# One layer of a hybrid encoder: the recurrence's products with T and with the scores as 64x64 tiles, the attention values as two 64-column products

## Chip, cores and metric

The kernel runs on one core of a Trainium2 chip. The metric is the device time of one execution in microseconds (us). The profile is of one execution of its own; times are the median of several runs without the profiler.

## What is computed

The layer takes a residual stream of 1024 tokens by 1024 features. One input projection feeds two groups of heads: neighbourhood attention (8 heads of 64) and a gated delta rule in both directions (4 heads of 128, chunks of 64 tokens). Their outputs go through one output projection, and a mixture of 64 small experts follows. The change lies in the last step of the delta rule and in the last product of the attention. The delta rule, for one direction and head, cut to what matters:

```python
def step(state, inp):                      # one chunk of 64 tokens, 16 chunks in turn
    q_c, k_c, u_c, w_c, g_c, qk_c = inp
    v_new = u_c - w_c @ state              # u_c, w_c: solutions of a triangular system
    o_c = (q_c * exp(g_c)) @ state + qk_c @ v_new
    state = state * exp(g_last) + (k_c * exp(g_last - g_c)).T @ v_new
    return state, o_c

out = einsum('bhqrc,rbhqce->bqhe', softmax(logits), v_win)   # attention values
```

## The kernel before

The work before the recurrence projects the inputs, convolves, builds for each of the 16 chunks the inverse T of the triangular matrix (64x64 for each head and direction, kept in DRAM as T_d) and the decayed scores (kept as SA_d). The recurrence then goes through 16 steps n. In step n the forward direction (d=0) takes chunk n and the backward one (d=1) takes chunk 15-n; tokens of d=0 lie on partitions 0 to 63, those of d=1 on partitions 64 to 127. The four heads h lie side by side in the columns.

One step (lines 509 to 567) does this:

- pk (line 529): keys and queries of the chunk times the state st, eight products of 128x128, four for each direction.
- r (line 531, VectorE): values minus the first half of pk, eight instructions on 64 partitions.
- pw (line 536): T times r, four products, one for each head. Both directions go in one product, so T stands in `at[:, 1, h]` as a 128x128 matrix with one 64x64 block for each direction on its diagonal and zeros elsewhere.
- wc (lines 537 and 538): the copy of pw out of PSUM, half by ScalarE, half by VectorE.
- ps (line 545): keys times wc, eight products that use 64 rows of the array each, rows 0 to 63 for d=0 and 64 to 127 for d=1.
- sn (lines 550 and 551): the old state is decayed by GpSimd and VectorE adds ps. This is the next state.
- po (line 559): the scores times wc, four products with the same block-diagonal form (`at[:, 0, h]`), into the buffer of pw. VectorE adds the part from the state (line 563) and GpSimd issues two transfers to on_d (line 565).

A matrix product of float32 operands is run as two passes, so the trace shows two MATMUL records for each of these products. Products of operands of the form float32r take one pass.

The program is written step after step, but a scheduler lays out each engine's instructions. Between the steps of the recurrence it puts the input projection of the other columns (nat_block, lines 84 to 86: three passes of 256 columns for each 128 rows, called fillers below). What is left of that projection follows the recurrence; then the attention begins.

The attention goes through 64 blocks of 128 queries of one head, two blocks (h=0, h=1) for each group of queries. attn_values (line 654 on) forms the product of the values with the transposed weights for both heads at once: the 128 columns of two heads as the stationary operand and 2x128 moving columns, three products summed. Only two of the four quarters of the result are used; two VectorE copies take them (line 665). The output projection (dn_mm2 and ao_mm, lines 84 to 86 again, with 512 columns) is laid between the attention's blocks by the scheduler.

Of the kernel before, what the change touches and what calls it, by code (L numbers as in the profile page):

```python
# [8 lines left out]
F32 = mybir.dt.float32  # L9
# [3 lines left out]
AF = mybir.ActivationFunctionType  # L13
OP = mybir.AluOpType
# [5 lines left out]
P = 128  # L20
# [5 lines left out]
DH, DD = 4, 128  # L26
CH = 64
NCH = S // CH
# [8 lines left out]
def tile_layer(ctx, tc, a, out):  # L37
    nc = tc.nc
    pe, act, dve, pool, sp = nc.tensor, nc.scalar, nc.vector, nc.gpsimd, nc.sync
# [137 lines left out]
    X, T1, T2, BETA, G, GC, EGC, DL, C1, C2 = (gt[:, i] for i in range(10))  # L177
    egl = dnp.tile([P, 2, NCH, DH], F32, name="egl")
# [322 lines left out]
    psK = scn.enter_context(tc.tile_pool(name="psK", bufs=1, space=PSUM, side="right"))  # L501
    hf = [slice(d * 64, d * 64 + 64) for d in range(2)]

    atb = [sc1.tile([P, 2, DH, 2, CH], F32, name=f"at{i}") for i in range(2)]
    for i in range(2):
        pool.memset(atb[i], 0.0)
    st = None
    for n in range(NCH):
        ch = [slice(step(d, n) * CH, step(d, n) * CH + CH) for d in range(2)]
        kn = sc2.tile([P, DH, DD], F32, name="kn")  # L510
        vn = sc2.tile([P, DH, DD], F32, name="vn")
        at = atb[n % 2]
        for d in range(2):
            sp.dma_start(at[hf[d], 1, :, d], T_d[hf[d], n])
            sp.dma_start(vn[hf[d]], v_d[ch[d]])
        for d in range(2):
            sp.dma_start(kn[hf[d]], k_d[ch[d]])
            sp.dma_start(at[hf[d], 0, :, d], SA_d[hf[d], n, :, 1])
        kd = sc2.tile([P, DH, DD], F32, name="kd")
        pool.tensor_tensor(kd, kn, DL[:, n, :, None].to_broadcast([P, DH, DD]), op=OP.mult)  # L520
# [12 lines left out]
        pw = psK.tile([P, DH, DD], F32, name="pw")  # L533
        wc = sc2.tile([P, DH, DD], F32, name="wc")
        for h in range(DH):
            pe.matmul(pw[:, h], at[:, 1, h], r[:, h], start=True, stop=True)
        act.activation(wc[:, 0:2], pw[:, 0:2], AF.Copy)
        dve.tensor_copy(wc[:, 2:4], pw[:, 2:4])
        if n < NCH - 1:
            sn = sc2.tile([P, 2, DH, DD], F32, name="sn")  # L540

            ps = [psK.tile([P, DH, DD], F32, name=f"ps{d}") for d in range(2)]
            for h in range(DH):
                for d in range(2):
                    pe.matmul(ps[d][:, h], kd[hf[d], h], wc[hf[d], h], start=True, stop=True)
            for d in range(2):
                if n == 0:
                    dve.tensor_copy(sn[:, d], ps[d])
                else:
                    pool.tensor_tensor(sn[:, d], st[:, d], egl[:, d, n, :, None].to_broadcast([P, DH, DD]), op=OP.mult)  # L550
                    dve.tensor_tensor(sn[:, d], ps[d], sn[:, d], op=OP.add)
        o = sc2.tile([P, DH, DD], F32, name="o")
        if n > 0:
            for h in range(DH):
                for d in range(2):
                    act.activation(o[hf[d], h], pk[d][hf[1], h], AF.Copy, scale=EGC[hf[d], n, h:h + 1])
        po = psK.tile([P, DH, DD], F32, name="pw")
        for h in range(DH):
            pe.matmul(po[:, h], at[:, 0, h].rearrange("p d c -> p (d c)"), wc[:, h], start=True, stop=True)
        if n == 0:  # L560
            dve.tensor_copy(o, po)
        else:
            dve.tensor_tensor(o, po, o, op=OP.add)
        for d in range(2):
            pool.dma_start(on_d[d, ch[d]], o[hf[d]].rearrange("p h e -> p (h e)"))
        if n < NCH - 1:
            st = sn

# [37 lines left out]
    qks, lgs, bts, pTs = {}, {}, {}, {}  # L606
# [47 lines left out]
    def attn_values(i):  # L654
        half, pr, w, h = blocks[i]
        if h == 0:
            return None

        pv, pT = psQ.tile([P, 2, P], F32, name="pv", bufs=1), pTs.pop(i // 2)
        for g in range(3):  # L660
            pe.matmul(pv, vw[:, w, half + g, pr * P:(pr + 1) * P], pT[:, g], start=(g == 0), stop=(g == 2))  # L661
        av = aTs[half][:, pr].rearrange("p (r c) -> p r c", c=64)[:, :, w * 16:w * 16 + 16]
        for h in range(2):
            hs = slice(h * 64, h * 64 + 64)
            ins = dve.tensor_copy(av[hs], pv[hs, h].rearrange("p (r c) -> p r c", c=16))
        return ins

    def attn_step(i):
        if i < len(blocks):
# [572 lines left out]
```

## Time and profile before

| | us |
|---|---|
| median of 3 runs | 1382.51 (1381.34 to 1383.73) |
| the profiled execution, its time | 1388.08 |
| its span from first to last instruction | 1386.4 |
| PE busy, share of the span | 85% |
| VectorE (DVE), GpSimd (POOL), ScalarE (ACT) busy | 46%, 28%, 27% |

Busy time is an average over stages with different limits. The recurrence lies between 345 and 490 us of the span, the rest of the input projection between 490 and 550, the attention with the output projection between 550 and 765, the router until 825, and the experts behind that. The rows below are from these stages.

### The profile page before, as it was taken

What the parts mean: (1) busy time and instruction counts of PE and PEld (TensorE: products, weight loads), DVE (VectorE), ACT (ScalarE), POOL (GpSimd) and SP (SyncE); (2) the same over time, 40 slices, a digit from 0 to 9 for tenths busy, and PEclk for the clock granted to TensorE, in tenths of its full rate; (3) what the DMA queues carried; (4) which work ended last, traced back from release to release, by engine and by line L of the source; (5) the groups of instructions that cost most, each with busy time, mean ns of one, the idle gap of its engine ahead of it and who ended that gap; (6) DMA issues with size and microseconds to landing.
All of it is one profiled execution on the core that took longest, in us unless ns stands there. A gap on an engine that the chain in (4) does not pass through costs nothing. (4 is left out here: it accounts for less than half of the span.)

```text
span 1386.4 us, 21032 instructions
## 1 busy us (share of the span) xinstructions
PE 1177.5 (85%) x7427; PEld 821.7 (59%) x7428; DVE 643.5 (46%) x1615; ACT 375.8 (27%) x768; POOL 381.9 (28%) x433
## 2 busy tenths in 40 slices
PE   6977999979989896679989968887887788868885
PEld 6866889979889895467768853333332333323332
DVE  5556863763466633667867962122211212122211
ACT  6435432322244423665545310000000000000000
POOL 1147313013567463121210352111212112212111
PEclk9989999988999997899999969999998999989999
DMA  4251246346666497998692979999999999998991
GB/s 160 67 116 48 66 143 166 97 135 137 198 184 163 124 251 199 261 266 206 166 265 104 334 307 357 398 409 400 398 404 397 353 391 406 393 372 333 402 383 54
DMA packets 109954, 347.13 MB, mean 250 GB/s; under 512 B 43104, under 2 KB 49248, under 8 KB 93168
## 3 DMA queue, kind: packets, MB, share of 16 engines
q1 hardware_dynamic: 74480, 260.68, 52.2%
q0 software_dynamic: 27056, 68.79, 19.2%
q10 hardware_dynamic: 8272, 15.78, 3.2%
q8 instruction: 83, 1.36, 0.4%
q14 instruction: 63, 0.52, 0.1%
HBM read 305.26 MB, written 61.67 MB: 265 GB/s over the span
## 5 line engine op out<-in xcount | busy, mean ns | idle before, releaser
L1037 PE MATMUL pp<-wg,xT 128*64 128x512 f32 x1024 | 229.7, 598 | 17.7 <-DVE xT L1026 16.7
L1072 PE MATMUL po<-wd,hT 128*64 128x512 f32 x512 | 128.2, 632 | 44.2 <-DVEq L1151 31.7
L1037 PEld LDWEIGHTS pp<-wg,xT 128*64 128x64 f32 x1024 | 72.3, 137 | 153.3 <-issue 130.4
L84 PE MATMUL pA<-w_hi,h_hi 128*128 128x256 f32 x512 | 151.2, 295 | 0.0
L86 PE MATMUL pA<-w_hi,h_lo 128*128 128x256 f32 x512 | 149.2, 291 | 0.0
L85 PE MATMUL pA<-w_lo,h_hi 128*128 128x256 f32 x512 | 148.9, 291 | 0.0
L1053 POOL DMA_INDIRECT out<-yg,tS x32 | 50.8, 1586 | 287.0 <-DVE yg L1074 243.3
L1041 DVE SCALAR_TENSOR_TENSOR sg<-pp,tS,sg 128x256 f32<-128x256 f32 x32 | 15.5, 484 | 229.9 <-ACTq L1151 185.8
L1072 PEld LDWEIGHTS po<-wd,hT 128*64 128x64 f32 x512 | 42.8, 144 | 129.9 <-issue 67.8
L1074 DVE TENSOR_SCALAR yg<-po,tS 128x512 f32<-128x512 f32 x64 | 46.7, 749 | 125.2 <-DMA out<-yg,tS 62.9
L84 PEld LDWEIGHTS pA<-w_hi,h_hi 128*128 128x128 f32 x512 | 101.1, 197 | 0.4 <-issue 0.2
L85 PEld LDWEIGHTS pA<-w_lo,h_hi 128*128 128x128 f32 x512 | 100.9, 197 | 0.0
L86 PEld LDWEIGHTS pA<-w_hi,h_lo 128*128 128x128 f32 x512 | 100.6, 196 | 0.1
L1040 ACT ACTIVATE sg<-pp,tS 128x256 f32<-128x256 f32 x32 | 15.1, 473 | 267.5 <-PE pp L1037 267.5
L84 PE MATMUL pA<-h_hi,w_hi 128*128 128x512 f32 x192 | 76.7, 399 | 0.0
L85 PE MATMUL pA<-h_lo,w_hi 128*128 128x512 f32 x192 | 76.6, 399 | 0.0
L86 PE MATMUL pA<-h_hi,w_lo 128*128 128x512 f32 x192 | 76.0, 396 | 0.0
L76 DVE TENSOR_TENSOR w_lo<-w_raw,w_hi 128x512 fp32r<-128x512 f32 x56 | 39.1, 714 | 72.6 <-ACT w_hi L75 71.0
L250 DVE SCALAR_TENSOR_TENSOR acc<-raw,convw,acc 128x1024 f32<-128x1024 f32 x48 | 63.2, 1319 | 11.5 <-ACT acc L248 11.1
L1049 ACT ACTIVATE hT<-ph 128x256 f32<-128x256 f32 x32 | 12.3, 384 | 193.4 <-PE ph L1047 193.4
L84 PE MATMUL pA<-wo_hi,t_hi 128*128 128x512 f32 x128 | 55.0, 429 | 7.1 <-ACT t_hi L746 5.3
L661 PE MATMUL pv<-pT,vw 128*128 128x256 f32 x192 | 54.3, 419 | 3.3 <-ACT pT L652 2.4
(338 smaller groups left out, 2329.4 us busy)
## 6 DMA issues: line engine op xcount, KB each, us to landing
wg<-in_w_gu SPq DMA_DIRECT2D x62, 2048.0 KB
wd<-in_w_down SPq DMA_DIRECT2D x63, 1024.0 KB
bt<-in_bias SPq DMA_DIRECT2D x24, 384.0 KB
w_raw<-in_w_nat SPq DMA_DIRECT2D x32, 256.0 KB
w_raw<-in_w_dn SPq DMA_DIRECT2D x24, 256.0 KB
k<-kk_d POOLq DMA_DIRECT2D x16, 384.0 KB
SA_d<-cm POOLq DMA_DIRECT2D x8, 512.0 KB
kk_d<-ev POOLq DMA_DIRECT2D x8, 512.0 KB
```

What stands on the lines that cost most here:

```text
L76: dve.tensor_sub(lo[:, k:k + 2], raw, hi[:, k:k + 2].bitcast(F32))
L84: pe.matmul(dst, sh, mh, start=(i == 0), stop=False)
L85: pe.matmul(dst, sh, ml, start=False, stop=False)
L86: pe.matmul(dst, sl, mh, start=False, stop=(i == n - 1))
L250: dve.scalar_tensor_tensor(acc, raw[:, t:t + S], convw[:, m, t:t + 1], acc, op0=OP.mult, op1=OP.add)
L661: pe.matmul(pv, vw[:, w, half + g, pr * P:(pr + 1) * P], pT[:, g], start=(g == 0), stop=(g == 2))
L1037: pe.matmul(pp[d * CAP:(d + 1) * CAP], xT[:, k, d * CAP:(d + 1) * CAP], ws[d][0][:, :, k * 256:(k + 1) * 256], start=(k == 0), stop=(k == ...
L1040: act.activation(sg[:n], pp[:n, 0], AF.Silu, scale=mf[:n, 3:4])
L1041: dve.scalar_tensor_tensor(sg[:n], pp[:n, 1], mf[:n, 3:4], sg[:n], op0=OP.mult, op1=OP.mult)
L1053: ins = pool.indirect_dma_start(out=out, out_offset=bass.IndirectOffsetOnAxis(ap=idx, axis=0), in_=yg, in_offset=None, bounds_check=S - 1, ...
L1072: pe.matmul(po[d * CAP:(d + 1) * CAP], hT[:, k, d * CAP:(d + 1) * CAP], w[1][:, k * D + c * 512:k * D + (c + 1) * 512], start=(k == 0), st ...
L1074: dve.tensor_scalar(yg[:n, cs], po[:n], mf[:n, 2:3], None, op0=OP.mult)
```

## The change

Three parts.

1. The products with T. T is loaded as it lies in DRAM into tt (one transfer for both directions), and each head and direction has a 64x64 product of its own. Even heads leave the result on the direction's own half of the partitions, odd heads on the other half (`hf[d ^ p]`). The result has two tiles, one for each direction, in two PSUM banks; ScalarE copies the one, VectorE the other. The block-diagonal buffers and their zeroing go.
2. As the odd heads now lie on the other half, the keys (four transfers of half the size in place of two), the scores (four in place of two) and the decay factors (DLs) are laid out so as well. The state products keep their form but are grouped by partition half i; the addition to the state becomes four instructions in place of two, that to o two in place of one, the transfers to on_d four in place of two. The products with the scores become eight of 64x64 in place of four.
3. attn_values forms one product for each head with 64 stationary columns and 128 moving ones, into the two halves of the partitions of one tile, and one copy in place of two.

```diff
-    atb = [sc1.tile([P, 2, DH, 2, CH], F32, name=f"at{i}") for i in range(2)]
-    for i in range(2):
-        pool.memset(atb[i], 0.0)
+    DLs = sc1.tile([P, 2, NCH, 2], F32, name="DLs")
+    for d in range(2):
+        for p in range(2):
+            dve.tensor_copy(DLs[hf[d ^ p], d], DL[hf[d], :, p::2])
...
         for d in range(2):
-            sp.dma_start(at[hf[d], 1, :, d], T_d[hf[d], n])
             sp.dma_start(vn[hf[d]], v_d[ch[d]])
         for d in range(2):
-            sp.dma_start(kn[hf[d]], k_d[ch[d]])
-            sp.dma_start(at[hf[d], 0, :, d], SA_d[hf[d], n, :, 1])
+            for p in range(2):
+                sp.dma_start(kn[hf[d ^ p], d], k_d[ch[d]][:, p::2])
+        for d in range(2):
+            for p in range(2):
+                sp.dma_start(at[hf[d ^ p], d], SA_d[hf[d], n, p::2, 1])
...
-        pw = psK.tile([P, DH, DD], F32, name="pw")
+        pw = [psK.tile([P, 2, DD], F32, name=f"ps{d}") for d in range(2)]
...
         for h in range(DH):
-            pe.matmul(pw[:, h], at[:, 1, h], r[:, h], start=True, stop=True)
-        act.activation(wc[:, 0:2], pw[:, 0:2], AF.Copy)
-        dve.tensor_copy(wc[:, 2:4], pw[:, 2:4])
+            g, p = divmod(h, 2)
+            for d in range(2):
+                pe.matmul(pw[d][hf[d ^ p], g], tt[hf[d], h], r[hf[d], h], start=True, stop=True)
+        act.activation(wc[:, 0], pw[0], AF.Copy)
+        dve.tensor_copy(wc[:, 1], pw[1])
...
-            ps = [psK.tile([P, DH, DD], F32, name=f"ps{d}") for d in range(2)]
-            for h in range(DH):
+            ps = [psK.tile([P, 2, 2, DD], F32, name=f"ps{1 + i}") for i in range(2)]
+            for g in range(2):
                 for d in range(2):
-                    pe.matmul(ps[d][:, h], kd[hf[d], h], wc[hf[d], h], start=True, stop=True)
+                    for i in range(2):
+                        pe.matmul(ps[i][:, d, g], kd[hf[i], d, g], wc[hf[i], d, g], start=True, stop=True)
...
-        po = psK.tile([P, DH, DD], F32, name="pw")
-        for h in range(DH):
-            pe.matmul(po[:, h], at[:, 0, h].rearrange("p d c -> p (d c)"), wc[:, h], start=True, stop=True)
+        po = [psK.tile([P, 2, DD], F32, name=f"ps{2 * i}") for i in range(2)]
+        for g in range(2):
+            for p in range(2):
+                for d in range(2):
+                    i = p ^ d
+                    pe.matmul(po[i][hf[d], g], at[hf[i], d, g], wc[hf[i], d, g], start=True, stop=True)
...
-        pv, pT = psQ.tile([P, 2, P], F32, name="pv", bufs=1), pTs.pop(i // 2)
+        pv, pT = psQ.tile([P, P], F32, name="pv", bufs=1), pTs.pop(i // 2)
         for g in range(3):
-            pe.matmul(pv, vw[:, w, half + g, pr * P:(pr + 1) * P], pT[:, g], start=(g == 0), stop=(g == 2))
+            for h in range(2):
+                hs = slice(h * 64, h * 64 + 64)
+                pe.matmul(pv[hs], vw[:, w, half + g, pr * P + h * 64:pr * P + h * 64 + 64], pT[:, g, h],
+                          start=(g == 0), stop=(g == 2))
```

The scheduler lays the new instructions out anew. On PE, in one step in the middle of the recurrence, the products with T stood so before (pw is their result, pA that of the fillers, and the size behind a name is that of the result):

```order
L536 MATMUL pw_3261<-r_3242,at0_2261 128x128
L84 MATMUL pA_4808<-w_hi_4512,h_hi_73 128x256
L536 MATMUL pw_3261<-r_3242,at0_2261 128x128
L85 MATMUL pA_4808<-w_lo_4513,h_hi_73 128x256
L536 MATMUL pw_3261<-r_3242,at0_2261 128x128 x2
L86 MATMUL pA_4808<-w_hi_4512,h_lo_74 128x256
L84 MATMUL pA_4808<-w_hi_4512,h_hi_73 128x256
```

The last six of the eight products with T of a step of the changed kernel (line 544; they go to ps0 for d=0 and ps1 for d=1), with the state product of line 555 and the score product of line 575 that stand between them:

```order
L544 MATMUL ps0_3108<-r_3089,tt_3074 64x128
L85 MATMUL pA_5072<-w_lo_4591,h_hi_73 128x256
L86 MATMUL pA_5072<-w_hi_4590,h_lo_74 128x256
L544 MATMUL ps1_3109<-r_3089,tt_3074 64x128
L86 MATMUL pA_5072<-w_hi_4590,h_lo_74 128x256
L84 MATMUL pA_5072<-w_hi_4590,h_hi_73 128x256
L85 MATMUL pA_5072<-w_lo_4591,h_hi_73 128x256
L544 MATMUL ps1_3109<-r_3089,tt_3074 64x128
L555 MATMUL ps2_3123<-wc_3110,kd_3087 128x128
L544 MATMUL ps1_3109<-r_3089,tt_3074 64x128
L575 MATMUL ps0_3149<-wc_3110,at_3075 64x128
L544 MATMUL ps1_3109<-r_3089,tt_3074 64x128
```

Products on the whole array, with fillers on the whole array between them, have become products on a quarter of it with the same fillers between them. Over the whole recurrence the 128 products with T (64 before) stand in 109 runs: 94 alone, 13 of two, 2 of four.

Behind the state products of the step, PE stood so before: four score products, and, with a filler between, the eight of the next step's pk.

```order
L545 MATMUL ps0_3199<-wc_3191,kd_3169 128x128
L545 MATMUL ps1_3200<-wc_3191,kd_3169 128x128
L559 MATMUL pw_3222<-wc_3191,at1_2262 128x128 x4
L86 MATMUL pA_4808<-w_hi_4512,h_lo_74 128x256
L529 MATMUL pk0_3243<-sn_3198,qkT_78 128x128 x4
L529 MATMUL pk1_3244<-sn_3198,qkT_78 128x128 x4
```

The same place of the changed kernel (pk is line 535 there):

```order
L555 MATMUL ps2_3030<-wc_3017,kd_2994 128x128
L575 MATMUL ps0_3056<-wc_3017,at_2982 64x128 x3
L84 MATMUL pA_5072<-w_hi_4590,h_hi_73 128x256
L535 MATMUL pk0_3090<-sn_3028,qkT_78 128x128
L85 MATMUL pA_5072<-w_lo_4591,h_hi_73 128x256
L86 MATMUL pA_5072<-w_hi_4590,h_lo_74 128x256
L84 MATMUL pA_5072<-w_hi_4590,h_hi_73 128x256
L85 MATMUL pA_5072<-w_lo_4591,h_hi_73 128x256
L86 MATMUL pA_5072<-w_hi_4590,h_lo_74 128x256
L535 MATMUL pk0_3090<-sn_3028,qkT_78 128x128 x2
L575 MATMUL ps2_3057<-wc_3017,at_2982 64x128 x4
L535 MATMUL pk0_3090<-sn_3028,qkT_78 128x128
```

The score products now stand in two groups, the second between the products pk of the next step. Counted over the recurrence, the 128 score products (64 before) stand in 16 runs of one, 15 of three, 15 of four and one of seven; the 120 state products, before in 15 runs of eight, stand in 14 of one, 14 of seven and one of eight. The number of places at which PE goes from products of one array shape to those of another is 30 before (128 rows by 128 columns to 64 by 128 and back, once in each of 15 steps) and 264 now: 206 between the whole array and 64x64, 14 from the whole array to 64x128, and 44 between 64x64 and 64x128.

In the attention, the value products of one group of queries stood so on PE before (pt are transposes, pq the logits, pA the output projection):

```order
L649 MATMUL pt_6783<-ident_60,lg_6640 128x128 x3
L661 MATMUL pv_6789<-pT_6650,vw_5082 128x256 x3
L635 MATMUL pq_6805<-k2_6466,q2_6465 128x384
L636 MATMUL pq_6805<-kl1_5100,q2_6465 128x384
L84 MATMUL pA_6895<-wo_hi_6730,t_hi_6799 128x512
```

A group of the changed kernel (line 681):

```order
L681 MATMUL pv_6915<-pT_6863,vw_5429 64x128
L84 MATMUL pA_6923<-wo_hi_5862,t_hi_6878 128x512
L85 MATMUL pA_6923<-wo_lo_5863,t_hi_6878 128x512
L84 MATMUL pA_6937<-wo_hi_5862,t_hi_6878 128x512
L681 MATMUL pv_6915<-pT_6863,vw_5429 64x128 x5
```

Three products of one run have become one and then five, with the output projection between. The 192 products (96 before, of 256 columns) stand in 59 runs, 25 of them of one product. Before, neither they nor their neighbours changed the array's shape; now PE goes to 128 rows by 64 columns and back 59 times.

## Rows read from the trace of the kernel before

**Rows 1.** Windows: busy us (count) by engine, granted clock, DMA share, GB/s.

```profile
345.00:490.00 145.00, 132.63 (x1200) 126.19 (x1200) 91.93 (x221) 56.95 (x162) 82.06 (x94) 0.95 0.61 167
...
550.00:765.00 215.00, 184.22 (x887) 147.10 (x887) 152.63 (x547) 124.55 (x267) 35.30 (x53) 0.91 0.81 214
```

**Rows 2.** Waits of PE and of DVE, 345 to 490: total, times, longest.

```profile
PE pk L529 <- DVE sn L551: 5.4, 4, 3.2
...
DVE wc L538 <- ACT wc L537: 14.2, 12, 2.2
```

**Rows 3.** Timeline of PE, one step: start, duration, operation, rows*columns of the array, count.

```profile
449.01 0.39 PE L536 MATMUL pw<-r,at 128*128 128x128 f32 x2
...
450.96 1.16 PE L545 MATMUL ps<-wc,kd 64*128 64x128 f32 x16
452.06 1.16 PE L559 MATMUL pw<-wc,at 128*128 128x128 f32 x8
453.05 1.97 PE L529 MATMUL pk<-sn,qkT 128*128 128x128 f32 x16
...
455.57 0.28 PE L85 MATMUL pA<-w_lo,h_hi 128*128 128x256 f32 x1
455.69 0.28 PE L86 MATMUL pA<-w_hi,h_lo 128*128 128x256 f32 x1
455.81 0.39 PE L536 MATMUL pw<-r,at 128*128 128x128 f32 x2
```

**Rows 4.** Timeline of PE, 450.7 to 451.0: from the fillers to ps.

```profile
450.75 0.28 PE L84 MATMUL pA<-w_hi,h_hi 128*128 128x256 f32 x1
450.96 0.38 PE L545 MATMUL ps<-wc,kd 64*128 64x128 f32 x2
```

**Rows 5.** Timeline of PE, 452.0 to 452.2: from ps to po.

```profile
451.74 0.38 PE L545 MATMUL ps<-wc,kd 64*128 64x128 f32 x3
452.06 0.38 PE L559 MATMUL pw<-wc,at 128*128 128x128 f32 x1
```

**Rows 6.** Timeline of PE, 453.0 to 453.1: from po to pk.

```profile
452.83 0.39 PE L559 MATMUL pw<-wc,at 128*128 128x128 f32 x2
453.05 0.29 PE L529 MATMUL pk<-sn,qkT 128*128 128x128 f32 x1
```

**Rows 7.** Timeline of PE at line 342 (64-column products): 195 to 206, beginning, end.

```profile
197.28 3.71 PE L342 MATMUL pB<-qkT 128*64 128x128 f32 x64
...
196.97 0.38 PE L261 MATMUL pB<-ident,acc 128*128 128x128 f32 x2
197.28 0.33 PE L342 MATMUL pB<-qkT 128*64 128x128 f32 x2
...
200.93 0.50 PE L84 MATMUL pA<-h_hi,w_hi 128*128 128x512 f32 x1
201.26 0.40 PE L85 MATMUL pA<-h_lo,w_hi 128*128 128x512 f32 x1
```

**Rows 8.** The value products: timeline of PE, and the copies (min/median/max ns).

```profile
714.86 1.46 PE L661 MATMUL pv<-pT,vw 128*128 128x256 f32 x6
...
L665 DVE COPY aT<-pv x64: 264/288/297, 555.0 to 761.9; 64x128 f32<-64x128 f32 x64
```

**Rows 9.** Groups, 345 to 490: count, busy us, mean ns, idle before.

```profile
L551 DVE TENSOR_TENSOR sn<-ps,sn 128x512 f32<-128x512 f32 x28 | 18.0, 684 | 8.0 <-PE ps L545 8.0
L538 DVE COPY wc<-pw 128x256 f32<-128x256 f32 x16 | 6.7, 422 | 14.2 <-ACT wc L537 14.2
...
L565 POOL DMA_DIRECT2D on_d<-o x32 | 17.6, 555 | 13.4 <-DVE o L563 6.7 <-issue 6.7
...
L514 SPq DMA_DIRECT2D at<-T_d x32: 573/600/688, 345.9 to 466.2; - x32
```

**Rows 10.** Windows around PE's longest idle time in the recurrence, columns as in Rows 1.

```profile
412.50:415.00 2.50, 0.13 (x1) 0.13 (x1) 1.48 (x3) 1.21 (x2) 0.04 (x1) 0.74 0.74 202
415.00:417.50 2.50, 2.50 (x12) 2.50 (x13) 1.52 (x4) 0.00 (x0) 2.50 (x3) 0.50 0.75 211
```

More of the change, by code (lines that the diff above doesn't have):

```diff
@@ L509, in tile_layer @@
         ch = [slice(step(d, n) * CH, step(d, n) * CH + CH) for d in range(2)]
-        kn = sc2.tile([P, DH, DD], F32, name="kn")
+        kn = sc2.tile([P, 2, 2, DD], F32, name="kn")
         vn = sc2.tile([P, DH, DD], F32, name="vn")
-        at = atb[n % 2]
+        tt = sc2.tile([P, DH, CH], F32, name="tt")
+        at = sc2.tile([P, 2, 2, CH], F32, name="at")
+        sp.dma_start(tt, T_d[:, n])
         for d in range(2):
-            sp.dma_start(at[hf[d], 1, :, d], T_d[hf[d], n])
             sp.dma_start(vn[hf[d]], v_d[ch[d]])
         for d in range(2):
-            sp.dma_start(kn[hf[d]], k_d[ch[d]])
-            sp.dma_start(at[hf[d], 0, :, d], SA_d[hf[d], n, :, 1])
-        kd = sc2.tile([P, DH, DD], F32, name="kd")
-        pool.tensor_tensor(kd, kn, DL[:, n, :, None].to_broadcast([P, DH, DD]), op=OP.mult)
+            for p in range(2):
[3 more added lines that the diff above has]
+                sp.dma_start(at[hf[d ^ p], d], SA_d[hf[d], n, p::2, 1])
+        kd = sc2.tile([P, 2, 2, DD], F32, name="kd")
+        pool.tensor_tensor(kd, kn, DLs[:, :, n, :, None].to_broadcast([P, 2, 2, DD]), op=OP.mult)
         if n == 0:
@@ L532, in tile_layer @@
                                              op0=OP.mult, op1=OP.add)
-        pw = psK.tile([P, DH, DD], F32, name="pw")
-        wc = sc2.tile([P, DH, DD], F32, name="wc")
+        pw = [psK.tile([P, 2, DD], F32, name=f"ps{d}") for d in range(2)]
+        wc = sc2.tile([P, 2, 2, DD], F32, name="wc")
         for h in range(DH):
-            pe.matmul(pw[:, h], at[:, 1, h], r[:, h], start=True, stop=True)
-        act.activation(wc[:, 0:2], pw[:, 0:2], AF.Copy)
-        dve.tensor_copy(wc[:, 2:4], pw[:, 2:4])
+            g, p = divmod(h, 2)
[3 more added lines that the diff above has]
+        dve.tensor_copy(wc[:, 1], pw[1])
         if n < NCH - 1:
             sn = sc2.tile([P, 2, DH, DD], F32, name="sn")
-            ps = [psK.tile([P, DH, DD], F32, name=f"ps{d}") for d in range(2)]
-            for h in range(DH):
+            ps = [psK.tile([P, 2, 2, DD], F32, name=f"ps{1 + i}") for i in range(2)]
+            for g in range(2):
                 for d in range(2):
-                    pe.matmul(ps[d][:, h], kd[hf[d], h], wc[hf[d], h], start=True, stop=True)
[L546 to L552, printed above, removed]
+                    for i in range(2):
+                        pe.matmul(ps[i][:, d, g], kd[hf[i], d, g], wc[hf[i], d, g], start=True, stop=True)
+            for i in range(2):
+                for d in range(2):
+                    sv = sn[:, d, d ^ i::2]
+                    if n == 0:
+                        dve.tensor_copy(sv, ps[i][:, d])
+                    else:
+                        pool.tensor_tensor(sv, st[:, d, d ^ i::2],
+                                           egl[:, d, n, d ^ i::2, None].to_broadcast([P, 2, DD]), op=OP.mult)
+                        dve.tensor_tensor(sv, ps[i][:, d], sv, op=OP.add)
+        o = sc2.tile([P, 2, 2, DD], F32, name="o")
         if n > 0:
@@ L555, in tile_layer @@
                 for d in range(2):
-                    act.activation(o[hf[d], h], pk[d][hf[1], h], AF.Copy, scale=EGC[hf[d], n, h:h + 1])
-        po = psK.tile([P, DH, DD], F32, name="pw")
-        for h in range(DH):
-            pe.matmul(po[:, h], at[:, 0, h].rearrange("p d c -> p (d c)"), wc[:, h], start=True, stop=True)
[L560 to L563, printed above, removed]
+                    act.activation(o[hf[d], h % 2 ^ d, h // 2], pk[d][hf[1], h], AF.Copy, scale=EGC[hf[d], n, h:h + 1])
+        po = [psK.tile([P, 2, DD], F32, name=f"ps{2 * i}") for i in range(2)]
+        for g in range(2):
+            for p in range(2):
+                for d in range(2):
+                    i = p ^ d
+                    pe.matmul(po[i][hf[d], g], at[hf[i], d, g], wc[hf[i], d, g], start=True, stop=True)
+        for i in range(2):
+            if n == 0:
+                dve.tensor_copy(o[:, i], po[i])
+            else:
+                dve.tensor_tensor(o[:, i], po[i], o[:, i], op=OP.add)
         for d in range(2):
-            pool.dma_start(on_d[d, ch[d]], o[hf[d]].rearrange("p h e -> p (h e)"))
+            for p in range(2):
+                pool.dma_start(on_d[d, ch[d]].rearrange("t (g p e) -> t p g e", g=2, p=2)[:, p], o[hf[d], p ^ d])
         if n < NCH - 1:
@@ L657, in attn_values @@
             return None
-        pv, pT = psQ.tile([P, 2, P], F32, name="pv", bufs=1), pTs.pop(i // 2)
+        pv, pT = psQ.tile([P, P], F32, name="pv", bufs=1), pTs.pop(i // 2)
         for g in range(3):
-            pe.matmul(pv, vw[:, w, half + g, pr * P:(pr + 1) * P], pT[:, g], start=(g == 0), stop=(g == 2))
+            for h in range(2):
+                hs = slice(h * 64, h * 64 + 64)
+                pe.matmul(pv[hs], vw[:, w, half + g, pr * P + h * 64:pr * P + h * 64 + 64], pT[:, g, h],
+                          start=(g == 0), stop=(g == 2))
         av = aTs[half][:, pr].rearrange("p (r c) -> p r c", c=64)[:, :, w * 16:w * 16 + 16]
[L663 to L666, printed above, removed]
+        return dve.tensor_copy(av, pv.rearrange("p (r c) -> p r c", c=16))
     def attn_step(i):
```

## Prediction, made before the changed kernel ran

> **What bounds the kernel now.** I read the windows first, to see which stages the change can reach. The recurrence lies in the stretch from 345 to 490 us, the attention in that from 550 to 765 [rows 1]. What follows is started by the attention's end and moves with it. In the recurrence TensorE (PE) is busy 132.6 of 145 us, VectorE (DVE) 91.9, GpSimd 82.1, ScalarE 57.0. So PE idles for only 12.4 us, although the recurrence is a chain of dependent steps: the scheduler has put fillers into the waits. In the attention PE is busy 184.2 of 215.
>
> The waits come next [rows 2]. PE's longest total is 5.4 us for the state. DVE's copy of wc waits 14.2 us in all for ScalarE's copy from the same tile, in 12 of 16 steps. The reader should see two candidates for what sets a step: PE's own sum of work, and the chain T, wc, state, pk, r.
>
> The timeline of one step decides between them [rows 3]. From 449.01 to 455.81 us, 6.80 us, PE runs 8 passes with T, 16 of ps, 8 of po, 16 of pk, and 16 fillers, the last at 455.69. Prices: neighbouring fillers start 0.12 apart; for 128 columns of float32 the last seven of po's eight passes take (1.16 - 0.38) / 7 = 0.11 each [rows 3, 5]. The 14 behind the first two of ps take (1.16 - 0.38) / 14 = 0.056 [rows 3, 4], because the two directions lie on different halves of the array's rows and run side by side. A run of k products whose two passes each share a tile, with neighbours on different tiles, therefore takes about (k + 1) x 0.11.
>
> One price is left, and the whole forecast hangs on it: what PE pays when the array's shape changes. By the ends of the records: the last filler ends at 451.03, and the first two passes of ps, on 64x128, at 451.34, 0.31 later [rows 4], where a pair would need 0.11. Ps ends at 452.12 and the first pass of po, on 128x128 again, at 452.44, 0.32 later [rows 5]. From po to pk, without a change of shape, it is 453.22 to 453.34, 0.12 [rows 6]. At the 64-column products of line 342, the first two end 0.26 behind the transposes before them; at the end it is 200.99 to 201.43, 0.44, where the next pass of 512 columns takes 0.23 [rows 7]. So a change costs 0.20 us, and 0.15 on the way into 64-column products. Now the step adds up: 16 x 0.12 + 8 x 0.11 + 9 x 0.11 + 8 x 0.11 + 16 x 0.11 + 2 x 0.20 = 6.83, against 6.80 measured. PE's own work fills this step.
>
> The Trainium skill says the same of the cause: its page "TensorEngine Tiling (Array Packing)", section "Key Properties", has "Mode switching requires drain", for a change of the tiling mode and not for a change of tile alone; the trace agrees, with 0.32 against 0.12.
>
> **The change part by part.** *Changes of shape in the recurrence.* Before 30, now 264, counted in PE's order: 234 more. At 0.20 each that is 46.8 us. For 44 of them, between 64x64 and 64x128, the trace has no row; free they would leave 190 x 0.20 = 38.0. I take 46.8, since all kinds that are shown pay. A product with T between two fillers now costs a change in, two passes and a change out, 0.62 us in place of 0.22, and the step has no idle time left that could hide it.
>
> *Passes in the recurrence.* T: before 128 passes x 0.11 = 14.1. Now 94 products alone x 0.22 + 13 pairs x 0.33 + 2 runs of four x 0.55 = 26.1: a product of a quarter of the size takes as long as a whole one when nothing stands beside it, and there are twice as many. Po: before 14.1; now 16 x 0.22 + 15 x 0.44 + 15 x 0.55 + 0.88 = 19.3. Ps: before 15 x 0.99 = 14.9; now 14 x 0.22 + 14 x 0.88 + 0.99 = 16.4. Together +18.7.
>
> *What PE's idle time takes up.* A longer step on PE gives the others more time, so waits shrink: 12.4 us at most, nothing at least. I take 9, since part of it stands at the recurrence's start and end.
>
> *A new wait.* One state product and one score product now stand between the last three products with T of d=1, and wait for ScalarE's wc of d=0; behind them on PE are the products for which the whole step waits. The copy takes about 0.42 us (DVE's of that size [rows 9]), and from the last T of d=0 to the first of them PE has three fillers and a T, 3 x 0.12 + 0.62. So nothing; if ScalarE is late by its other work, its lateness counts in each step.
>
> *The other engines in the recurrence.* The addition to the state becomes 56 instructions of 128x256 in place of 28 of 684 ns; at 422 ns, the row of that size, +4.5 us, and the one to o likewise +2.5 [rows 9]. DVE had 53 us to spare. The transfers to on_d double: 32 more x 555 ns = 17.8 us on GpSimd, which had 63 to spare; behind them wait the decay of the state and kd, the next step's work. SP issues 11 transfers a step in place of 8, 48 more x 600 ns = 28.8 us over a stretch that gets longer; the fillers' weights (line 74) stand in the same queue, loaded a block ahead. ScalarE's wc no longer holds DVE's back, as the halves lie in two tiles. That frees up to 14.2 us of the chain, but not of PE, which has work then. All of this is covered by PE's step; without that cover it would be 6.8 on DVE less 14.2.
>
> *Attention.* Passes: before 192 x (1.46 - 0.38) / 5 = 0.216 [rows 8], 41.5 us. Now (192 + 59) x 0.11 = 27.6 (line 342 does 64 passes in 3.71 us, 0.055 each, the same shape [rows 7]). That saves 13.9. The changes of shape take 59 x (0.20 + 0.15) = 20.7. PE: +6.8. DVE loses 32 copies of 288 ns, 9.2 us, and PE does wait for DVE here. Between -9 (PE's idle hides the rest) and +6.8 I take +2.
>
> **Sum.** 46.8 + 18.7 - 9 + 2 = 58.5. The profiled execution took 1388.1 us, so 1446.6. The median of the runs before, 1382.5, is 5.6 lower, and the same shift gives 1441. By the bounds: 38.0 + 18.7 - 12.4 - 9 = +35, 1418; 46.8 + 18.7 + 6.8 = +72, 1455.
>
> **Rivals.** *Faster: the step is set by the chain, and the changes of shape are free beside it.* For it speaks DVE's wait of 14.2 for ScalarE, now gone, and that PE did wait in some steps. Then 18.7 - 12.4 - 13.9 - 14.2 = -22, 1361. It decides where a change of shape costs less than 22 / 352 = 0.06 us (234 in the recurrence, 118 in the attention). Against it: every change in rows 4, 5 and 7 costs at least 0.15, and the step of 6.80 has no idle time in it.
>
> *Four tiles at once.* If the 64x64 products ran four side by side, T and po would take 2 x 256 / 4 x 0.11 = 14.1 in place of 28.2, and with free changes and the attention's 13.9 the time would be near 1382.5 - 14.1 - 13.9 = 1354.5. The order speaks against it: only 34 of the 128 products with T stand beside another one at all. I give this 1 in 100. The Trainium skill, "TensorEngine Tiling (Array Packing)", section "Available Configurations", lists four independent tiles for 64x64; no run here shows four of them in flight.
>
> *Half hidden.* If waits for r, wc or the state fall just before the changes, half of them cost nothing: 23.4 + 18.7 - 9 - 3.6 = +30, 1412.
>
> *Slower still, by the clock.* After PE had been idle for 4 us, the granted clock fell to 0.50, the lower of the two levels, for about 5 us [rows 10]. If the many stops let it fall in a fifth of the recurrence, then some 185 us long, half of 37 us is lost: 1460. Against it: in the dense steps with two changes each it stood at the upper level.
>
> **How the numbers follow.** My forecast 0.78, half hidden 0.08, the clock 0.06, faster 0.05 in all, no change by a sum in between 0.03. The likeliest gives 1441. The range runs from the half hidden case to some way past the clock's: 1405 to 1470. Within 0.2% of the time before is about what a measurement can tell from no change. Slower by more: 0.92; within: 0.03; faster: 0.05.
>
> **What would show it.** In the changed trace a lone product with T between fillers should end 0.3 us behind the filler before it, and the next filler 0.3 behind that; a step should take about 10 us; PE should show no idle time in the recurrence; the attention should last as long as before within 8 us. I am wrong if 64x64 products run beside whole ones, if a step stays near 7 us, or if the copies and additions on DVE, or the transfers on SP, are what PE then waits for.

## The result: 1429.0 us, 3.0% slower, and the profile after

The changed kernel took 1429.01 us, the median of 4 runs (1416.08 to 1435.5), against 1382.69 for the kernel before (4 runs). The ratio is 1.0298, with a 95% interval of 1.0255 to 1.034. The profiled execution took 1431.07 us, its span is 1429.4, 43.0 longer than before, and its mean clock 0.936 (before 0.938).

The first and last instructions of three lines say where the time went. The columns are count, the shortest, median and longest duration, the starts of the first and the last, and the shape.

```profile
L544 PE MATMUL ps<-vn,tt x16: 269/269/320, 358.4 to 359.8; 64*64 64x128 f32 x16
...
L575 PE MATMUL ps<-wc,at x256: 269/269/473, 362.5 to 540.1; 64*64 64x128 f32 x128
...
L681 PE MATMUL pv<-pT,vw x384: 272/273/477, 595.4 to 798.8; 128*64 128x128 f32 x192
```

Before, the first product with T (line 536) began at 360.7, the last score product (line 559) at 486.4, and the value products (line 661) lay between 552.7 and 761.2. So the recurrence went from 126 to 182 us. Some fillers that used to stand behind it moved into it; from the first T to the first value product it is 192.0 before and 237.0 now. **All of the loss lies there, +45 us.** The attention went from 208.5 to 203.4. What follows it took 5 us more. That last stretch took between 625 and 634 us in all the traces of this study, without an order that follows the edits, so I read nothing from it.

The windows (columns as in [rows 1]) show the changed kernel's recurrence, then the stretch from the first T to the first value product, in the changed kernel and in the kernel before.

```profile
358.00:540.00 182.00, 176.76 (x1325) 133.87 (x1327) 94.10 (x260) 54.55 (x158) 101.06 (x145) 0.92 0.45 119
...
358.40:595.40 237.00, 219.72 (x1656) 174.48 (x1655) 114.89 (x316) 67.08 (x180) 132.06 (x183) 0.91 0.58 147
...
360.70:552.70 192.00, 167.32 (x1393) 158.73 (x1394) 109.71 (x275) 68.09 (x182) 107.12 (x122) 0.92 0.71 182
```

In the recurrence PE is busy for 176.8 of 182 us; DVE and GpSimd have 80 us and more to spare. Over the longer stretch PE is busy 52 us more than before and idles 17.3 us in place of 24.7. The granted clock is 0.92 in the recurrence.

The waits in the recurrence (waiting line, what it waited for: total, times, longest):

```profile
DVE wc L546 <- PE ps L544: 41.6, 16, 4.5
...
PE pk L535 <- DVE sn L564: 3.1, 2, 1.6
...
PE ps L544 <- DVE r L537: 1.0, 1, 1.0
```

DVE's wait for ScalarE's copy [rows 2] is gone. Now DVE waits for PE. PE waits for almost nothing.

One step on PE's timeline, 451.89 to 462.62, is 10.73 us long where that of [rows 3] had 6.80:

```profile
451.89 0.43 PE L544 MATMUL ps<-r,tt 64*64 64x128 f32 x2
452.25 0.38 PE L85 MATMUL pA<-w_lo,h_hi 128*128 128x256 f32 x1
452.57 0.43 PE L544 MATMUL ps<-r,tt 64*64 64x128 f32 x2
452.93 0.39 PE L86 MATMUL pA<-w_hi,h_lo 128*128 128x256 f32 x1
453.15 0.28 PE L84 MATMUL pA<-w_hi,h_hi 128*128 128x256 f32 x1
453.26 0.28 PE L85 MATMUL pA<-w_lo,h_hi 128*128 128x256 f32 x1
453.47 0.44 PE L544 MATMUL ps<-r,tt 64*64 64x128 f32 x4
...
455.55 0.48 PE L555 MATMUL ps<-wc,kd 64*128 64x128 f32 x2
455.96 0.32 PE L544 MATMUL ps<-r,tt 64*64 64x128 f32 x1
455.97 0.32 PE L575 MATMUL ps<-wc,at 64*64 64x128 f32 x1
455.97 0.42 PE L544 MATMUL ps<-r,tt 64*64 64x128 f32 x2
456.13 0.27 PE L575 MATMUL ps<-wc,at 64*64 64x128 f32 x1
...
460.19 0.61 PE L535 MATMUL pk<-sn,qkT 128*128 128x128 f32 x4
460.73 0.65 PE L575 MATMUL ps<-wc,at 64*64 64x128 f32 x8
461.31 1.38 PE L535 MATMUL pk<-sn,qkT 128*128 128x128 f32 x10
462.62 0.43 PE L544 MATMUL ps<-r,tt 64*64 64x128 f32 x4
```

Read the ends. A filler ends at 452.25 + 0.38 = 452.63, the lone product with T at 453.00, 0.37 later, and the next filler at 453.32, 0.32 behind that. The two together take 0.69, where without a change of shape they would take 0.22 + 0.12 = 0.34. So, by this reading of the ends, the way into 64x64 costs 0.15, the way out 0.20. The two products of 453.47 also end 0.37 behind the filler before them: two on different quarters of the array take the time of one. From 455.96 two products with T and one with the scores, on three quarters, again end 0.37 behind what stands before them. PE shows no idle time in the step. It holds 23 fillers, where the one before held 16.

### The profile page after: what moved, and what is told of

The parts are those of the page before. It is cut to its first block, busy times and chain, and to the rows that moved or that the text cites. A ratio compares the mean times of both kernels' runs of the same rounds, so it can differ in the third digit from the quotient of the medians.

```text
span 1429.4 us, 22107 instructions
## 1 busy us (share of the span) xinstructions
PE 1230.3 (86%) x7875; PEld 828.1 (58%) x7876; DVE 635.8 (44%) x1633; ACT 372.1 (26%) x766; POOL 404.8 (28%) x491
## 5 line engine op out<-in xcount | busy, mean ns | idle before, releaser
L1055 PE MATMUL pp<-wg,xT 128*64 128x512 f32 x1024 | 233.2, 607 | 21.4 <-DVE xT L1044 21.0
L76 DVE TENSOR_TENSOR w_lo<-w_raw,w_hi 128x512 fp32r<-128x512 f32 x56 | 40.6, 737 | 67.1 <-ACT w_hi L75 65.3
L1067 ACT ACTIVATE hT<-ph 128x256 f32<-128x256 f32 x32 | 12.3, 384 | 192.0 <-PE ph L1065 176.6
L569 ACT ACTIVATE o<-pk,gt 64x128 f32<-64x128 f32 x120 | 35.6, 358 | 80.7 <-PE pk L535 43.8
```

The costliest lines, as they stand in the source:

```text
L76: dve.tensor_sub(lo[:, k:k + 2], raw, hi[:, k:k + 2].bitcast(F32))
L569: act.activation(o[hf[d], h % 2 ^ d, h // 2], pk[d][hf[1], h], AF.Copy, scale=EGC[hf[d], n, h:h + 1])
L1055: pe.matmul(pp[d * CAP:(d + 1) * CAP], xT[:, k, d * CAP:(d + 1) * CAP], ws[d][0][:, :, k * 256:(k + 1) * 256], start=(k == 0), stop=(k == ...
```

## The experiments

In each, the kernel before was run on the same chip, and a ratio is to it.

**The attention's part alone.** The kernel before with the last part of the diff:

```diff
-            pe.matmul(pv, vw[:, w, half + g, pr * P:(pr + 1) * P], pT[:, g], start=(g == 0), stop=(g == 2))
+            for h in range(2):
+                hs = slice(h * 64, h * 64 + 64)
+                pe.matmul(pv[hs], vw[:, w, half + g, pr * P + h * 64:pr * P + h * 64 + 64], pT[:, g, h], ...
```

> The kernel before with the third part alone (attention values as 64-column products, 118 changes of the array's shape in the attention, none more in the recurrence). My account puts the loss into the recurrence: the attention's passes save 13.9 us, the changes cost 118 halves of about 0.35, some of it in PE's idle time, and the trace of the changed kernel shows the attention about 7 us shorter: 1372 to 1384 us. Rival, that the attention bears a good part of the loss: above 1395.

Measured: 1385.89 us (12 runs) against 1386.97, 0.9998 (0.998 to 1.0016). No change: neither the gain that I expected nor the rival's loss. The attention takes 207 us.

**The recurrence's parts alone.** The changed kernel with the attention of before:

```diff
-        pv, pT = psQ.tile([P, P], F32, name="pv", bufs=1), pTs.pop(i // 2)
+        pv, pT = psQ.tile([P, 2, P], F32, name="pv", bufs=1), pTs.pop(i // 2)
...
+            pe.matmul(pv, vw[:, w, half + g, pr * P:(pr + 1) * P], pT[:, g], start=(g == 0), stop=(g == 2))
```

> The changed kernel with the attention values as before (parts 1 and 2 alone). My account: all of the loss, 1425 to 1445 us. Rival as in the run with the attention alone: below 1410.

Measured: 1431.66 us, 1.0327 (1.0287 to 1.0368). The whole loss is the recurrence's.

**All eight products with T in one run.** The changed kernel, with each product behind the last r in PE's order (here and below, behind sets the order in which instructions are issued and nothing else):

```diff
+                m = pe.matmul(pw[d][hf[d ^ p], g], tt[hf[d], h], r[hf[d], h], start=True, stop=True)
+                if n > 0:
+                    behind(m, last_r)
```

> The changed kernel with the eight products with T of a step laid in one run behind the last r: the same products, transfers and instructions on every engine, the same three tiles, but 116 changes of shape in the recurrence in place of 264, and T starts later in the step. My account (changes of shape): 148 x 0.17 = 25 us less, and 11 less for passes that now run side by side, so 1385 to 1403. Rival, that twice as many products cost it by their number: 1418 (the passes alone). Rival, that the added work on VectorE, GpSimd and SyncE costs it: no change, 1429, or slower by the later start.

Measured: 1421.9 us, 1.0261 (1.0232 to 1.0291). This missed; the trace shows where the gain went. PE's timeline, the products with T of two steps:

```profile
446.93 0.32 PE L85 MATMUL pA<-w_lo,h_hi 128*128 128x256 f32 x1
447.18 0.67 PE L549 MATMUL ps<-r,tt 64*64 64x128 f32 x16
...
455.97 0.67 PE L549 MATMUL ps<-r,tt 64*64 64x128 f32 x16
```

PE's longest wait in its recurrence:

```profile
PE pk L540 <- DVE sn L571: 13.3, 8, 2.3
```

And the window from its first T to its first value product:

```profile
358.40:584.00 225.60, 193.26 (x1655) 168.15 (x1654) 113.38 (x316) 67.09 (x180) 131.60 (x183) 0.86 0.62 153
```

Sixteen passes now start within 0.67 - 0.27 = 0.40 us, 0.027 apart, a quarter of the 0.11 of a whole pass. A step without a wait takes 447.18 to 455.97, 8.79 us, with 23 fillers, 1.94 less than above; 15 steps would save 29. But the products now wait for the slowest r, the state comes later, and PE waits 13.3 us for it, 10.2 more than before this edit. From the first T to the first value product it is 225.6 us, 11.4 less than in the changed kernel: PE is busy 26 us less there and idles 15 us more (32.3 against 17.3). The granted clock is 0.86 over 226 us against 0.91 over 237: (0.14 x 225.6) - (0.09 x 237.0) = 10 us of full clock less, which stand in the busy time. So at the full clock PE's work fell by up to 36 us, the 25 + 11 that were expected, and idle time and clock took 25 of them back. The total is 7 us less, and the intervals of the two ratios overlap.

**The products with T in pairs.** To tell the price of the changes from what that grouping brought along, only the two directions' products of one head were put side by side:

```diff
-            for d in range(2):
-                pe.matmul(pw[d][hf[d ^ p], g], tt[hf[d], h], r[hf[d], h], start=True, stop=True)
+            for d in (1, 0):
+                m = pe.matmul(pw[d][hf[d ^ p], g], tt[hf[d], h], r[hf[d], h], start=True, stop=True)
+                if d:
+                    first = m
+                else:
+                    behind(m, first)
```

> The changed kernel, with the two directions' products with T of one head put side by side in PE's order: the one of d=0 may not go ahead of the one of d=1. No instruction is added or left out; of the 264 changes of shape in the recurrence 166 remain. Theory (PE pays for each lone run of 64x64 products: 0.14 us in and 0.195 out, and two passes): 98 changes at 0.167 and about 7 us of passes are gone, 23 us of PE's work, and no product waits for anything it did not wait for before the change was made, so 1400 to 1412 us. Rival (what the grouping of all eight products showed: the chain of a step or the clock takes most of it back, whatever PE saves): 1418 to 1427 us. Rival that the number of changes is not the cause: 1427 to 1433.

Measured: 1400.99 us, 1.0094 (1.0068 to 1.012), as the theory said. PE's timeline has two products where there was one, and they end at the same 0.37 behind the filler:

```profile
396.06 0.28 PE L85 MATMUL pA<-w_lo,h_hi 128*128 128x256 f32 x1
396.27 0.44 PE L549 MATMUL ps<-r,tt 64*64 64x128 f32 x4
```

The window from its first T to its first value product:

```profile
358.40:563.90 205.50, 183.76 (x1647) 154.80 (x1647) 115.95 (x315) 67.33 (x180) 131.42 (x182) 0.93 0.64 168
```

98 changes fewer go with 28 us less. At 0.175 each, the mean of the two ways, they are 17 us. The passes that now run side by side (7 by the expectation) and the clock (0.93 over 205.5 us where it was 0.91 over 237.0, up to 7) cover the rest; the run by itself does not tell the three apart.

**More whole products, no change of shape.** The kernel before with four more products with T in a step:

```diff
+                    if d == 0:
+                        behind(pe.matmul(pw[:, h], at[:, 1, h], vn[:, h], start=True, stop=True), m)
```

> The kernel before with four more products with T in each of 15 steps, whole ones (128x128), one behind each r of d=0, where the changed kernel has its 64x64 products of d=0. They work on vn in place of r, and the real products then overwrite them: the output is the same. No change of shape is added; passes of T in the recurrence go from 128 to 248. Theory (the shape is what costs): 120 passes at 0.11 us, 13 us of PE's work, of which waits take up some: 0 to 13 us over the kernel before. Rival (more and shorter runs of products cost, whatever their shape, as in the changed kernel): 25 to 45 us over it.

Measured: 1391.42 us, 1.0045 (1.0026 to 1.0065), 6 us. So it is not the number of products. The windows show PE busy for 96% of the recurrence, at the full clock throughout:

```profile
358.00:490.00 132.00, 126.47 (x1141) 119.92 (x1139) 84.89 (x210) 51.48 (x153) 76.54 (x88) 1.00 0.57 155
```

**Without fillers, before and after.** The projections were held back until the last score product, in both kernels; the same edit in each:

```diff
             m = pe.matmul(dst, sh, mh, start=(i == 0), stop=False)
+            if late is not None:
+                behind(m, late)
```

> The kernel before, with the projections that the scheduler had put between the steps of the recurrence (L84 to L86, about 250 products and their turns) held back until the last product with the scores. Nothing is left out. PE then waits for the chain in each step, and the step shows the chain's own length. Theory: a step of 5.0 to 6.0 us in place of 6.8, the recurrence 80 to 95 us, the held work 30 to 40 us behind it; total 1375 to 1395. Rival (a step is set by the chain already, fillers cost nothing): a step stays at 6.5 to 7.5 us and the total goes up by the held work, 1410 or more.

> The changed kernel with the same projections held back until the last product with the scores; 119 changes of shape remain in the recurrence, and PE has no other work there. Theory (the loss is PE's: changes between fillers and lone products): the recurrence is within 15 us of that of the kernel before without fillers, and the total within 20 us of it, 1385 to 1410. Rival (the chain itself got longer, by the transfers, the halved instructions on DVE or GpSimd, or slower 64x64 products): the recurrence is over 30 us longer than that of the kernel before without fillers, total 1415 or more.

Measured: 1440.79 us (1.0391, 1.0373 to 1.0408) and 1491.66 us (1.0739, 1.0719 to 1.0759). More was held back than I meant, also from the stretch ahead of the recurrence, so the totals say little; the steps do. A step of the kernel before without fillers on PE's timeline, from one T to the next (in brackets PE's idle time ahead of the row and what ended it):

```profile
404.82 1.27 PE L543 MATMUL pw<-r,at 128*128 128x128 f32 x8 [0.69 <-DVE r L538]
...
406.87 1.16 PE L552 MATMUL ps<-wc,kd 64*128 64x128 f32 x16 [0.77 <-ACT wc L544]
...
411.60 1.27 PE L543 MATMUL pw<-r,at 128*128 128x128 f32 x8 [0.70 <-DVE r L538]
```

The windows over this step and over the recurrence:

```profile
404.82:411.60 6.78, 5.31 (x49) 4.84 (x49) 4.56 (x13) 2.76 (x11) 4.09 (x6) 1.00 0.61 159
...
341.00:451.00 110.00, 87.06 (x741) 79.45 (x742) 69.24 (x182) 41.75 (x136) 60.34 (x74) 0.95 0.54 143
```

The step takes 6.78 us with PE busy for 5.31. With 16 fillers it took 6.80 [rows 3]. **The rival was right on this point: the chain alone is as long as the step with fillers, and PE's work only just fitted into it.** The changed kernel without fillers, the part of a step between pk and ps on PE's timeline:

```profile
425.69 1.28 PE L542 MATMUL pk<-sn,qkT 128*128 128x128 f32 x6
426.90 0.65 PE L582 MATMUL ps<-wc,at 64*64 64x128 f32 x8
427.49 1.38 PE L542 MATMUL pk<-sn,qkT 128*128 128x128 f32 x10
...
431.76 1.16 PE L562 MATMUL ps<-wc,kd 64*128 64x128 f32 x14 [0.52 <-DVE wc L553]
```

Its windows, over a step at the full clock, one at the lower level, and the recurrence:

```profile
433.59:441.50 7.91, 6.96 (x65) 5.26 (x65) 4.84 (x16) 2.76 (x9) 5.61 (x10) 1.00 0.46 114
...
466.90:479.03 12.13, 11.09 (x65) 8.76 (x64) 4.84 (x15) 2.75 (x10) 5.60 (x9) 0.50 0.24 67
...
342.00:503.00 161.00, 143.12 (x993) 112.15 (x994) 73.11 (x226) 41.69 (x136) 82.91 (x132) 0.66 0.38 102
```

The chain of the changed kernel takes 7.9 us at the full clock, 1.1 longer, against my expectation of no great difference between the two; over 15 steps that is 17 of the 50 us by which the recurrences without fillers differ. The rest goes with the clock: 0.66 over 161 us against 0.95 over 110. A step at the lower level takes 4.2 us more. So recurrence and total lie in the rival's range, more by the clock than by the chain. In the longer step PE is busy for 6.96 us in place of 5.31 and idles for 0.95 in place of 1.47: what was added is work of PE, not longer waits.

**The order of pk and po in that chain.** In the timeline above four score products stand between the two parts of pk, with two changes of shape; r waits for them. So pk was held behind all score products, as in the kernel before:

```diff
+                    behind(pe.matmul(pk[d][:, h], qkT[:, h, step(d, n)], st[:, d, h], start=True, stop=True), *pos)
```

> The changed kernel without projections in the recurrence, with the state's products pk held behind all score products po, as in the kernel before: 89 changes of shape where there were 119. Theory (in the chain without fillers, four score products and two changes of shape stood between the two directions' pk, and made the step 7.90 us long where that of the kernel before without fillers took 6.78): at the upper clock a step takes 6.7 to 7.3 us. Rival (the chain is longer by the 64x64 products, the halved additions or the transfers): 7.7 us or more. On the clock: in the kernel before without fillers it stood at the upper level through the recurrence, in the changed one without fillers it was low in over half of it; if that belongs to the 64x64 products, it is low here too for over a third of the recurrence; if it belonged to the order, it is not.

Measured: 1500.0 us, in one run. No step came near 7 us. The windows over the shortest, and over one at the lower level throughout:

```profile
374.11:382.88 8.77, 6.99 (x67) 5.44 (x65) 4.85 (x15) 2.76 (x9) 6.14 (x11) 0.94 0.52 133
...
447.80:460.30 12.50, 10.87 (x66) 8.72 (x64) 4.85 (x15) 2.76 (x9) 5.62 (x10) 0.50 0.30 84
```

At 0.50 the step is 12.50 where it was 12.13: putting pk behind did not shorten the chain. It is no clean test of the order, though, for the edit brought a wait of its own: PE now waits ahead of the second score products, 6.6 us in 11 steps by the list of waits. Their tile is one of the two into which the state products were written, and DVE's additions must have read it; that this is the wait is not shown. Which of PE's products make the chain 1.1 us longer stays open. The clock was low in most of the recurrence here too, 0.68 over 164 us, so the order of pk and po does not make it fall.

**What of the change can be kept.** T's result in two tiles, in the kernel before, so that DVE's copy does not wait for ScalarE's:

```diff
-        pw = psK.tile([P, DH, DD], F32, name="pw")
+        pw = [psK.tile([P, 2, DD], F32, name=f"ps{i}") for i in range(2)]
```

> The kernel before, with the result of the products with T in two tiles, so that VectorE's copy of wc no longer waits for ScalarE's (14.2 us in all); nothing else, but the scheduler now puts two of the eight state products ahead, so that the shape changes 58 times in the recurrence and not 30. My account (PE's own work fills the step): 28 x 0.20 = 5.6 us slower, 1383 to 1390. Rival (the chain sets the step): up to 14 us faster, 1369 to 1376.

Measured: 1382.24 us (12 runs), 0.9969 (0.9949 to 0.9988): 4 us less, between the two accounts. The window from its first T to its first value product:

```profile
357.70:551.10 193.40, 174.92 (x1401) 163.07 (x1399) 111.94 (x281) 69.29 (x186) 107.54 (x123) 0.96 0.73 192
```

Its recurrence, from the first T to the last score product, takes 118 us where it took 126, so the wait of 14.2 us [rows 2] was on the chain. But 195 fillers stand in it where there were 252; the others now follow it, and up to the first value product it is 193.4 us, 1.4 more than before. **A shorter chain gained nothing there: the fillers that no longer fit between the steps are PE's work behind them.** The 4 us lie elsewhere. In this trace the attention took 201 us, with the code that took 208.5 before; in the five traces with that code it took between 198 and 211, so a few us of it say nothing of an edit.

Then the attention's part with its six value products in one run, the one that is ready last issued first:

```diff
+            for h in (1, 0):
...
+                if g == 0 and h == 1:
+                    first = m
+                else:
+                    behind(m, first)
```

> The kernel before with the attention of the change alone, its six value products put into one run: 76 changes of shape where the attention of the change alone had 118. Theory: the changes were what ate the gain of the attention part; 42 fewer at about 0.17 us give 7 us, and the shorter run lets PE go on to the next block's products: 6 to 14 us under the kernel before. Rival (most of the gain of the kernel with split wc and grouped attention came from the split): within 4 us of the kernel before.

Measured: 1382.65 us (12 runs) against 1386.55, 0.9968 (0.9951 to 0.9984): 4 us, so the rival's side. And both together:

> The kernel before, with the result of T in two tiles (so that DVE's copy of wc does not wait for ScalarE's) and with the attention of the change, its six value products grouped into one run (76 changes of shape in place of 118). Theory: the split gives 4 us as measured, the attention part measured as no change with 118 changes, and 42 changes fewer give 42 x 0.17 = 7: 1370 to 1376 us. Rival (PE's time in the attention is hidden by the waits for pT, mx and aT): 1378 to 1383, the split's gain alone.

Measured: **1370.52 us (5 runs) against 1387.63, 0.9872 (0.9853 to 0.9891), faster than both kernels by more than its parts add up to.** The windows over the attention show it, first with the attention's part alone, 118 changes:

```profile
548.00:756.00 208.00, 178.63 (x1060) 132.52 (x1059) 136.38 (x510) 117.72 (x259) 35.31 (x53) 0.90 0.82 220
```

With the products in one run, 76 changes:

```profile
552.00:757.00 205.00, 172.72 (x1067) 131.34 (x1066) 137.25 (x508) 119.65 (x259) 35.08 (x53) 0.89 0.83 224
```

With 76 changes and the two tiles:

```profile
553.00:739.00 186.00, 166.10 (x1061) 126.36 (x1061) 135.00 (x502) 116.90 (x257) 34.98 (x53) 0.93 0.86 236
```

From the first to the second PE's busy time fell by 6 us and the stretch by 3, from the second to the third they fell by 7 and by 19. The third, 186 us, lies under anything that the attention took without the two edits together. PE's wait for DVE's maximum of the logits is 15.3 us in 11 times in the second and 6.6 in 6 in the third, and the clock is higher: (0.11 x 205) - (0.07 x 186) = up to 10 of the 19 us. Why the two edits help each other was not settled.

## Why the prediction was right, and where its steps were off

**What set the step** was argued wrongly. The sum of PE's work, 6.83 against 6.80, was taken as proof that PE sets it. Without fillers it takes 6.78: both limits stood at the same place, and a sum that fits did not tell them apart. It was also a dense step: in 8 of the 14 steps of that trace PE idles, once for 3.2 us. The conclusion held for a reason that the prediction does not have: fillers that find no room between the steps follow the recurrence, so what counts is PE's work up to the first value product. T in two tiles made the recurrence 8 us shorter and this stretch no shorter; 13 us of whole passes made the stretch 10 us longer (202.1) and the kernel 6.

**The changes of shape**, with the lone passes that go with them, were the right cause, shown by the pairs (98 fewer, 28 us less) and by the whole products (none, 6 us). How much of the loss is the changes and how much the passes is worked out from the ends of the records. The term of 46.8 was mis-sized: 125 of the changes lead into 64x64 and cost 0.15, the others 0.20, so (125 x 0.15) + (139 x 0.20) - (30 x 0.20) = 40.6. The attention's way in had been priced at 0.15 from [rows 7]; it holds for 64x64 too. "All kinds that are shown pay" was right.

**The passes**, +18.7, came out at about half. The formula let a run of two take 0.33 and counted T and po beside each other as lone. In the step above, three of them end 0.37 after what stands before, as one does: 2 x 0.22 less per step, 6.6 us; a pair saves 0.11, 1.4; the four of po at 460.73 end 0.58 behind pk, 0.43 without the way in, where the formula has 0.55, 1.8. Left are 9. "Four tiles at once" had 1 in 100, and the order did keep the products apart, as was said against it. The array can do it: in one run four tiles work side by side, 0.027 us per pass. The Trainium skill, "TensorEngine Tiling (Array Packing)", section "Available Configurations", lists four independent tiles for 64x64; the run of sixteen passes agrees.

**The idle time.** From the first T to the first value product PE idled 24.7 us before and 17.3 after. I took up 9; it was 7.4.

**The clock** was a rival at 0.06, and it fell beside what was forecast, though not only behind idle time, from which the rival was priced (the last section). That idle time was 3.2 us [rows 2], not 4. The clock of 0.91 over 237.0 us against 0.92 over 192.0 cost at most (0.09 x 237.0) - (0.08 x 192.0) = 6 us. Together 40.6 + 9 - 7.4 + 6 = 48; measured were 45. The 3 us left are not explained. So 1441 came near 1429 in part by luck: the changes were put 6 too high and the passes 10, while the clock was not in the sum.

**The other engines** were covered, as said: PE waited 1.0 us for r and 3.1 for the state. The new wait for wc of d=0 cost nothing: it is not in PE's list of waits. **Attention:** forecast +2, measured -5 in the profile, less than the attention varied by without an edit to it (198 to 211 us), and no change in the run alone. PE's records of the value products fell from 54.3 to 42.5 us in spite of the changes, but the time did not follow.

**By the list of what would show it:** the lone product ends 0.37 behind the filler and the filler 0.32 behind that (0.3 each was said); the step takes 10.7 (about 10); PE idles 5.2 of 182 us; the attention stayed within 8 us. None of the three signs against the forecast appeared.

## What to carry to other kernels

A product on a part of the array costs what its neighbours make of it: sixteen passes of 64x64 in one run started 0.027 us apart, where whole passes take 0.11 each, and one product between whole-array products took two and a half times as long as a whole one in its place (0.57 us against 0.22). Put products of one shape side by side before making them smaller, and count changes of shape in the engine's order rather than in the code. Where filler work has been packed into a chain, PE's sum and the chain may be equally long; take the fillers out to see which is. And where fillers can move behind the chain, a shorter chain is worth nothing until the stretch that ends with the last filler gets shorter.

## What the runs showed of the hardware that was not expected

The granted clock fell while PE was busy. Three windows of the changed kernel; the second is the end of the first:

```profile
482.00:491.60 9.60, 9.60 (x48) 7.42 (x48) 4.80 (x14) 1.30 (x5) 5.45 (x9) 0.68 0.59 138
488.20:491.60 3.40, 3.40 (x18) 2.00 (x17) 1.43 (x4) 0.94 (x4) 0.00 (x0) 1.00 0.78 180
491.60:501.80 10.20, 10.20 (x54) 8.09 (x56) 2.77 (x7) 2.71 (x8) 4.01 (x7) 0.50 0.35 96
```

At 491.6 it fell from the upper level, 1.00, to the lower, 0.50, after 9.6 us without idle time, in a stretch of 64x64 products between fillers. The two other falls in this recurrence have idle time at hand: the one at 372.1 came 1.8 us after PE had idled for 0.99 us, the one at 481.4 while PE idled for 1.57 us. Without fillers the clock was 0.66 with PE busy for 89% of the recurrence and no wait over 0.6 us (from 355 to 500), where the kernel before had 0.95 with 79%, and 1.00 from 350 to 440 with waits of up to 0.8; with more whole products it was 1.00 at 96%. The Trainium skill, "TensorE: Matmul & The Clock Gate", section "HAM oscillation — how this bites in real kernels", ties such falls to gaps in PE's work; here the busier kernels had the lower clock, so the measurement decides: being busy with these products did not hold the clock up. Which property of these products does it was not separated.
